# Row pads that shift the start bytes of operand tiles in a hybrid decoder trunk

## The chip, the cores and the metric

The kernel runs on one core of one Trainium2 chip, as one launch. The metric is the device time of that launch in microseconds, the median over repeated executions.

## The reference

Two layers (DEPTH 2) over 512 positions of width 1024, float32. Each layer computes an RMSNorm, one combined input projection, three groups of heads side by side (6 heads of differential attention, 4 groups of a short gated convolution, 6 heads of RWKV-7 time mixing), one output projection added to x, then a second RMSNorm and a squared-ReLU MLP of width 4096, added to x. A final RMSNorm follows.

```python
for l in range(DEPTH):
    h = rms_norm(x, norm_mix_g[l])
    proj = h @ w_in[l]
    p_att, p_conv, p_rwkv = jnp.split(proj, [3 * ATT_W, 3 * ATT_W + 3 * CONV_W], axis=-1)
    ...
    mixed = jnp.concatenate([o_att, o_conv, o_rwkv], axis=-1)
    x = x + mixed @ w_out[l]
    h = rms_norm(x, norm_mlp_g[l])
    x = x + jnp.square(jax.nn.relu(h @ w_mlp_up[l])) @ w_mlp_down[l]
return rms_norm(x, final_norm_g)
```

## The kernel before

x is held transposed, as 8 tiles `x[j]` of 128 partitions (features) by 512 positions. Every large product is taken at float32 precision in three matmuls: the weight block and the activation are each split into a rounded part (`hi`, type float32r) and a remainder (`lo`), and the product is whi x ahi + whi x alo + wlo x ahi (the function `mm3_steps`, and `passes` in the mixer). The activation is the moving operand of the matmul, 512 wide; the weight block of 128 x 128 is the stationary one. The split costs a copy on ACT and a subtraction on DVE or POOL for each weight half group (256 KB, loaded by SP's queue into `raw`) and each activation tile.

Stages of one layer, with the names that the profile uses:

- **Mixer.** `entry` (layer 1: also `scaled`, lines 401 to 407) writes the scaled input tiles `ahim`/`alom`. `products` runs the 26 groups of the input projection into `pj`. Attention (`sc`, `ptt`), RWKV (`pw`, `pa<-za`, `pg`, `pzw`, `pap` and others) and convolution are generators; a written-out list (ORDER) says which generator takes its next step, and this is the order on every engine. Matmuls of `pj` are put between the small matmuls of attention and RWKV. The decay products `pw` take the tiles `tw`, `to` as moving operands and `lkt`, `lvt` as weights. Results go to the mixed tiles `mhi`/`mlo` 0 to 7 (`mix_out`, line 846). The output projection `po` takes them in the order `K_ORD = (0, 5, 3, 1, 6, 4, 2, 7)` in two cuts of four: for each of the 8 output tiles first the tiles 0, 5, 3, 1, amid attention and RWKV work, and later, for each output tile, 6, 4, 2, 7, as one long stream.
- **Start of the MLP.** `inputs` writes `ahif`/`alof`, and the up projection `up` starts: 3 blocks within the mixer's list, then blocks up to 8.
- **MLP.** Of the 32 up blocks, 8 are plain (`up`) and 24 are taken as 12 pairs by the function `two`, which uses a 2 x 2 block scheme with 7 products instead of 8 (each 256 wide, 4 blocks deep, 12 matmuls): three of the products have as moving operand parts of the normed input (`bhi`/`blo`), four have combinations of them, the block tiles `thi`/`tlo`. The squared-ReLU results are the middle tiles `mh`/`ml`, in rings of 10, which the down projection `dn` (and `dnF` in the last group of layer 1) takes as moving operands. The order in this stage is the scheduler's, from the order in which the program is written.

All SBUF tiles come from pools that lay one tag behind the other, padded to 32 bytes per partition; tiles of one tag share a slot of the largest size. The map of the built program before the change (bytes within a partition):

| tiles | first start | step | start modulo 512 |
|---|---|---|---|
| `x0` to `x7` | 1,600 | 2,048 | 64 |
| tags `ahi0`, `alo0`, `ahi1`, ... `alo7`: `ahim`/`alom`, `mhi`/`mlo` of tiles 1, 2, 3, 4, 6, 7, `ahif`/`alof`, `bhi`/`blo` | 23,424 | 2,048 | 384 |
| `raw`, `whi`, `wlo` | 61,312 | 2,048 | 384 |
| `mh` ring, then `ml` ring | 98,176 | 2,048 | 384 |
| `thi0` to `tlo3`, with other tiles between | 163,712 | 4,096 and more | 384 |
| `tw`, `to`, `lkt`, `lvt` of layer 0 | 129,952 | 2,048 | 416 |
| mixed tiles 0 and 5 of layer 0 ("own" home, in the mixer's pool) | 210,336 and 216,480 | - | 416 |
| mixed tiles 0 and 5 of layer 1 | 218,528 and 212,320 | - | 416 and 352 |

The mixer's pool (`mp`) and the MLP's pool (`fp`) take turns in the same memory from 83,840 on; the mixer's ends at 228,800 before the change.

Of the kernel before, what the change touches and what calls it, by code (L numbers as in the profile page):

```python
# [11 lines left out]
F32R = mybir.dt.float32r  # L12
# [10 lines left out]
S = 512  # L23
P = 128
# [255 lines left out]
def tile_trunk(ctx: ExitStack, tc: tile.TileContext, xT, wts, prm_d, cst_d, lora_d, gup_d, lam_d, fin_d, out):  # L280
# [20 lines left out]
    cp = Pool(ctx.enter_context(tc.tile_pool(name="cp", bufs=1)), "cp")  # L301
# [119 lines left out]
    def got(d, k):  # L421

        while k not in d:
            yield
        return d[k]
# [4 lines left out]
    def entry(ready, l):  # L430

        for j in range(NK - LATE if l else 0, NK):
            yield from got(ready, ("x", j))
            gcol = prm[l][:, C_GMIX + j:C_GMIX + j + 1]
            hi = cp.tile([P, S], F32R, tag=f"ahi{j}", name=f"ahim{l}_{j}")
            lo = cp.tile([P, S], F32R, tag=f"alo{j}", name=f"alom{l}_{j}")
            acts[j] = (hi, lo)
            yield act.activation(hi, x[j], AF.Identity, scale=gcol)
            yield dve.scalar_tensor_tensor(lo, x[j], gcol, hi.bitcast(F32), ALU.mult, ALU.subtract)
# [132 lines left out]
    for l in range(L):  # L572
# [5 lines left out]
        with ExitStack() as mx:  # L578
# [652 lines left out]
            def att_pair(t):  # L1231
# [106 lines left out]
                for b in range(NB):  # L1338
# [6 lines left out]
            work = {"d": loads(), "w": casts(), "x": rests(dve), "y": rests(pool), "m": products(), "o": outputs(),  # L1345
                    "n": norm(), "g": rates(), "h": gate(), "i": inputs(), "p": squares(), "N": inner_norm()}
            work |= {"e": entry(ready, l), "q": entry_norm(ready, l)}
            if l == 0:
                work["k"] = constants(ready)
# [13 lines left out]
        with ExitStack() as mx:  # L1363
            fp = mx.enter_context(tc.tile_pool(name=f"fp{l}", bufs=1))
            RING = 10
            H = S // 2
# [4 lines left out]
            def kept(m):  # L1371

                i = len(mids)
                hi = fp.tile([P, S], F32R, tag="mh", bufs=RING, name=f"mh{l}_{i}")
                lo = fp.tile([P, S], F32R, tag="ml", bufs=RING, name=f"ml{l}_{i}")
                act.copy(hi, m)  # L1376
                pool.tensor_tensor(lo, m, hi.bitcast(F32), ALU.subtract)  # L1377
                mids.append((hi, lo))

            def square(cs, name):  # L1380

                r = fp.tile([P, S], F32, tag="r", bufs=2, name=f"r{name}")
                for i, c in enumerate(cs):
                    act.activation(r[:, i * H:i * H + c.shape[1]], c, AF.Relu)
                m = fp.tile([P, S], F32, tag="m", bufs=3, name=f"m{name}")
                act.activation(m, r, AF.Square)
                kept(m)
# [14 lines left out]
            bn, th = {}, {}  # L1402
# [6 lines left out]
            def blocks(k):  # L1409
                b1, b2 = bn[k], bn[k + 4]  # L1410
                t = [fp.tile([P, 2, H], F32, tag=f"s{2 * (k % 2) + i + 1}", name=f"t{l}_{k}_{i}") for i in range(2)]
                dve.tensor_tensor(t[0][:, 0], b1[:, 1], b1[:, 0], ALU.subtract)
                dve.tensor_tensor(t[0][:, 1], b2[:, 1], t[0][:, 0], ALU.subtract)
                dve.tensor_tensor(t[1][:, 0], b2[:, 1], b1[:, 1], ALU.subtract)
                dve.tensor_tensor(t[1][:, 1], b2[:, 0], t[0][:, 1], ALU.subtract)
                hi, lo = th[k] = [fp.tile([P, 4, H], F32R, tag=f"t{p}{k}", name=f"t{p}{l}_{k}") for p in ("hi", "lo")]
                for i in range(2):
                    u = slice(2 * i, 2 * i + 2)
                    act.copy(hi[:, u], t[i])
                    dve.tensor_tensor(lo[:, u], t[i], hi[:, u].bitcast(F32), ALU.subtract)  # L1420
# [89 lines left out]
            for i in range(N_ONE):  # L1510
                up(i)
                for j in range(2 * max(i - 2, 0), min(2 * max(i - 1, 0), NK)):
                    scaled_by_norm(j)
                if i >= N_ONE - 4:
                    blocks(i - N_ONE + 4)
# [79 lines left out]
```

## Time and profile before

| | |
|---|---|
| median of 3 runs | 1267.0 us (1266.56 to 1267.16) |
| profiled execution, its own time | 1266.47 us |
| its span, first to last instruction | 1264.7 us |
| mean granted clock of TensorE | 0.998 |
| PE busy | 1242.8 us, 9493 matmuls |
| DVE busy | 913.5 us |
| ACT busy | 696.9 us |
| POOL busy | 335.3 us |

The page lists instruction groups by line, engine, operation and tiles; all matmuls have the line of one helper (L289), so that they are told apart by their tiles (`dn<-ml,whi`: output, moving operand, weights). Matmuls overlap in the pipe: the duration of one is longer than the distance from its start to the next start, and it is the latter that adds up.

### The profile page before, as it was taken

How to read it: one execution, taken by the hardware profiler on the slowest of the kernel's cores; microseconds unless marked ns; L12 is line 12 of the kernel's file. 1: busy time of each engine (PE TensorE's matmuls, PEld its weight loads, DVE VectorE, ACT ScalarE, POOL GpSimd, SP SyncE). 2: the span in 40 equal slices, each digit the busy share in tenths (PEclk: the TensorE clock that was granted, in tenths of full speed). 3: DMA queues.
4: the chain of work that ended last, by engine and by line, in shares of the span. 5: the costliest groups of instructions: out<-in, count | busy, mean ns of one | idle time of the engine just before them, and what ended most of it. 6: DMA issues, size and time to landing. Idle time of an engine off the chain costs nothing.

```text
span 1264.7 us, 25145 instructions
## 1 busy us (share of the span) xinstructions
PE 1242.8 (98%) x9493; PEld 1051.4 (83%) x9493; DVE 913.5 (72%) x1889; ACT 696.9 (55%) x1474; POOL 335.3 (27%) x433
## 2 busy tenths in 40 slices
PE   9999999999999999999999999999999999999997
PEld 6777777787789898989878787787787989898987
DVE  6788888867966666765667787879598666666654
ACT  7675655646744544544575656564575545454553
POOL 1353626133300101010224335352431010111110
PEclk9999999999999999999999999999999999999999
DMA  6522333142333333321235333332424233333122
GB/s 212 159 84 94 109 94 101 52 134 83 103 122 101 101 101 100 101 84 51 75 103 146 98 102 110 98 97 60 134 92 133 93 107 96 106 98 103 59 74 77
DMA packets 84410, 127.93 MB, mean 101 GB/s; under 512 B 21440, under 2 KB 25024, under 8 KB 84288
## 3 DMA queue, kind: packets, MB, share of 16 engines
q1 hardware_dynamic: 83568, 125.77, 32.6%
q8 instruction: 75, 1.23, 0.4%
q10 hardware_dynamic: 720, 0.55, 0.1%
q14 instruction: 47, 0.39, 0.1%
HBM read 117.11 MB, written 9.18 MB: 100 GB/s over the span
## 4 chain that ended last, share of the span: by engine, by line
PE 70%; DVE 4%; issue 1%; ACT 1%; DMA 0%; POOL 0%; DVEq 0%; ACTq 0%; POOLq 0%
PE dn L289 22%; PE pj L289 11%; PE pa L289 11%; PE up L289 6%; PE pb L289 5%; PE po L289 4%; PE dnF L289 3%; PE pc L289 3%; PE sc L289 1%; PE ptt L294 1%; PE pg L289 1%; DVE wlo L343 0%; DVE blo L1429 0%; DVE x L1505 0%; PE pyy L289 0%
## 5 line engine op out<-in xcount | busy, mean ns | idle before, releaser
L1377 POOL TENSOR_TENSOR ml<-m,mh 128x512 fp32r<-128x512 f32 x64 | 95.2, 1489 | 510.8 <-ACT mh L1376 510.6
L342 ACT CAST whi<-raw 128x512 fp32r<-128x512 f32 x142 | 88.1, 621 | 174.1 <-PE dn L289 158.5
L289 PE MATMUL dn<-mh,whi 128*128 128x512 f32 x448 | 175.3, 391 | 1.9 <-DVE x L1505 1.9
L289 PE MATMUL dn<-ml,whi 128*128 128x512 f32 x448 | 174.6, 390 | 0.0
L289 PE MATMUL dn<-mh,wlo 128*128 128x512 f32 x448 | 174.4, 389 | 0.0
L289 PE MATMUL pj<-ahim,whi 128*128 128x512 f32 x392 | 157.7, 402 | 4.4 <-DVE vf L1266 1.7
L289 PE MATMUL pj<-ahim,wlo 128*128 128x512 f32 x392 | 158.3, 404 | 0.0
L289 PE MATMUL pj<-alom,whi 128*128 128x512 f32 x392 | 158.2, 404 | 0.0
L662 ACT CAST whi<-raw 128x512 fp32r<-128x512 f32 x142 | 87.7, 619 | 93.6 <-PE pj L289 40.4
L671 POOL TENSOR_TENSOR wlo<-raw,whi 128x512 fp32r<-128x512 f32 x62 | 81.7, 1317 | 214.5 <-ACT whi L662 198.3
L1505 DVE TENSOR_TENSOR x<-dn,x 128x512 f32<-128x512 f32 x112 | 76.8, 686 | 76.8 <-PE dn L289 76.8
L343 DVE TENSOR_TENSOR wlo<-raw,whi 128x512 fp32r<-128x512 f32 x142 | 115.2, 812 | 11.4 <-ACT whi L342 10.7
L1444 DVE TENSOR_TENSOR slo_p<-s,shi_p 128x512 fp32r<-128x512 f32 x96 | 70.9, 740 | 63.6 <-ACT shi_p L1443 58.9
L289 PEld LDWEIGHTS dn<-mh,whi 128*128 128x128 f32 x448 | 84.2, 188 | 21.3 <-ACT whi L342 2.4
L289 PEld LDWEIGHTS dn<-mh,wlo 128*128 128x128 f32 x448 | 84.1, 188 | 17.8
L289 PEld LDWEIGHTS dn<-ml,whi 128*128 128x128 f32 x448 | 84.2, 188 | 16.5
L289 PEld LDWEIGHTS pj<-ahim,whi 128*128 128x128 f32 x392 | 73.9, 188 | 19.8 <-issue 1.7
L1443 ACT CAST shi_p<-s 128x512 fp32r<-128x512 f32 x96 | 59.2, 618 | 51.2 <-PE pa L289 39.1
L289 PEld LDWEIGHTS pj<-ahim,wlo 128*128 128x128 f32 x392 | 73.8, 188 | 14.3 <-issue 0.9
L289 PEld LDWEIGHTS pj<-alom,whi 128*128 128x128 f32 x392 | 73.8, 188 | 14.1 <-issue 0.5
L289 PE MATMUL pa<-thi,shi_p 128*128 128x256 f32 x288 | 81.6, 283 | 0.2 <-DVE c L1489 0.2
L289 PE MATMUL pa<-thi,slo_p 128*128 128x256 f32 x288 | 81.5, 283 | 0.0
(409 smaller groups left out, 3264.5 us busy)
## 6 DMA issues: line engine op xcount, KB each, us to landing
raw<-wts SPq DMA_DIRECT2D x391, 256.0 KB, 2.7
qs<-dqhi SPq DMA_DIRECT2D x24, 128.0 KB, 3.3
ks<-dkhi SPq DMA_DIRECT2D x24, 128.0 KB, 3.8
x<-xT SPq DMA_DIRECT2D x8, 256.0 KB, 5.0
dqhi<-qhi SPq DMA_DIRECT2D x6, 256.0 KB, 3.3
dqlo<-qlo SPq DMA_DIRECT2D x6, 256.0 KB, 2.8
dkhi<-khi SPq DMA_DIRECT2D x6, 256.0 KB, 2.6
dklo<-klo SPq DMA_DIRECT2D x6, 256.0 KB, 2.9
```

The lines of the kernel that those rows point to most:

```text
L289: ins = nc.tensor.matmul(*a, **k)
L294: ins = nc.tensor.transpose(*a, **k)
L342: act.copy(hi[:, :n], raw[:, :n])
L343: (pool if a and lean[0] else dve).tensor_tensor(lo[:, :n], raw[:, :n], hi[:, :n].bitcast(F32), ALU.subtract)
L662: yield act.copy(hi[:, k0:k1], raw[:, k0:k1])
L671: yield eng.tensor_tensor(lo[:, :n], raw[:, :n], hi[:, :n].bitcast(F32), ALU.subtract)
L1377: pool.tensor_tensor(lo, m, hi.bitcast(F32), ALU.subtract)
L1443: act.copy(hi, src)
L1444: dve.tensor_tensor(lo, src, hi.bitcast(F32), ALU.subtract)
L1505: dve.tensor_tensor(x[j], pt, x[j], ALU.add)
```

## The change

Three kinds of tiles get a pad at the end of each row, and a view without the pad is used in their place. Shapes, values, instructions and their order as written stay.

- The input tiles `ahim`/`alom` written by `entry` have 520 elements, 2,080 bytes (were 512 and 2,048). Their tags `ahi0` to `alo7` are shared by all tiles of the second row of the table above, and a slot has the size of its largest tile.
- The middle tiles `mh`/`ml` have 528 elements, 2,112 bytes.
- The block tiles `thi`/`tlo` have 1,040 elements, 4,160 bytes (were 1,024 and 4,096).

```diff
@@ entry
-            hi = cp.tile([P, S], F32R, tag=f"ahi{j}", name=f"ahim{l}_{j}")
-            lo = cp.tile([P, S], F32R, tag=f"alo{j}", name=f"alom{l}_{j}")
+            hi = cp.tile([P, S + 8], F32R, tag=f"ahi{j}", name=f"ahim{l}_{j}")[:, :S]
+            lo = cp.tile([P, S + 8], F32R, tag=f"alo{j}", name=f"alom{l}_{j}")[:, :S]
@@ kept
-                hi = fp.tile([P, S], F32R, tag="mh", bufs=RING, name=f"mh{l}_{i}")
-                lo = fp.tile([P, S], F32R, tag="ml", bufs=RING, name=f"ml{l}_{i}")
+                hi = fp.tile([P, S + 16], F32R, tag="mh", bufs=RING, name=f"mh{l}_{i}")[:, :S]
+                lo = fp.tile([P, S + 16], F32R, tag="ml", bufs=RING, name=f"ml{l}_{i}")[:, :S]
@@ blocks
-                hi, lo = th[k] = [fp.tile([P, 4, H], F32R, tag=f"t{p}{k}", name=f"t{p}{l}_{k}") for p in ("hi", "lo")]
+                hi, lo = th[k] = [fp.tile([P, 4 * H + 16], F32R, tag=f"t{p}{k}", name=f"t{p}{l}_{k}")[:, :4 * H].rearrange("p (i s) -> p i s", s=H)
+                                  for p in ("hi", "lo")]
```

## The prediction

> **What bounds the kernel now.** I read the page first, then the groups with shapes kept apart, the waits of PE, the chain, and the timeline of PE alone around the second layer's output projection.
>
> ```profile
> span 1264.7 us, 25145 instructions
> PE 1242.8 (98%) x9493; PEld 1051.4 (83%) x9493; DVE 913.5 (72%) x1889; ACT 696.9 (55%) x1474; POOL 335.3 (27%) x433
> PEclk9999999999999999999999999999999999999999
> 369.47 10.91 PE dn L289 x48
> ...
> PE ptt L294 <- DVE pp L1311: 2.7, 4, 0.9
> ...
> 335.00:632.00 297.00, 295.78 (x1774) 1.00 0.30 94
> 632.00:908.00 276.00, 272.99 (x2712) 1.00 0.36 106
> 908.00:954.00 46.00, 45.85 (x209) 1.00 0.29 92
> ...
> L289 PE MATMUL dn<-mh,whi 128*128 128x512 f32 x448 | 175.3, 391 | 1.9 <-DVE x L1505 1.9
> L289 PE MATMUL dn<-ml,whi 128*128 128x512 f32 x448 | 174.6, 390 | 0.0
> L289 PE MATMUL dn<-mh,wlo 128*128 128x512 f32 x448 | 174.4, 389 | 0.0
> ```
>
> PE is busy 98% of the span, at full granted clock. The chain's piece of 48 down matmuls takes 10.91 us, 227 ns from start to start, with nothing between them; the stretches (layer 0's MLP, layer 1's mixer, layer 1's first up projections) have 295.78 of 297 us, 272.99 of 276 and 45.85 of 46 covered. PE's longest group of waits for another engine sums to 2.7 us. So the end is set by what one matmul costs PE; a change of addresses counts if it alters that, and otherwise hardly at all. Busy durations overlap (389 to 391 ns of one `dn` matmul at a pitch of 227), so I go by start times.
>
> **Does the start byte of a moving operand alter it?** The trace has no addresses, but the old map has a natural experiment. Nearly every operand of the long streams starts at 384 modulo 512, a multiple of 64. The exceptions include the mixed tiles 0 and 5 of layer 1 (own home: 416 and 352) and the decay inputs `tw`, `to` with their weights (416): 32 past a multiple of 64. In `po` the order of tiles is 0, 5, 3, 1, three matmuls each. Here is PE's timeline (start us, duration us):
>
> ```profile
> 876.32 0.39 PE L289 MATMUL po<-mhi,whi 128*128 128x512 f32 x1
> ...
> 877.71 0.40 PE L289 MATMUL po<-mhi,whi 128*128 128x512 f32 x1
> ...
> 879.10 0.40 PE L289 MATMUL po<-mhi,whi 128*128 128x512 f32 x1
> 879.34 0.39 PE L289 MATMUL po<-mlo,whi 128*128 128x512 f32 x1
> ...
> 880.47 0.40 PE L289 MATMUL po<-mhi,whi 128*128 128x512 f32 x1
> ...
> 881.64 0.40 PE L289 MATMUL po<-mhi,wlo 128*128 128x512 f32 x1
> ```
> ```profile
> 35.87 0.39 PE L289 MATMUL pj<-ahim,whi 128*128 128x512 f32 x1
> 36.10 0.40 PE L289 MATMUL pj<-alom,whi 128*128 128x512 f32 x1
> 36.33 0.39 PE L289 MATMUL pw<-tw,lkt 128*128 128x512 f32 x1
> 36.56 0.39 PE L289 MATMUL pw<-to,lvt 128*128 128x512 f32 x1
> 36.79 0.39 PE L289 MATMUL pj<-ahim,wlo 128*128 128x512 f32 x1
> ...
> 37.48 0.39 PE L289 MATMUL pj<-ahim,wlo 128*128 128x512 f32 x1
> 37.71 0.39 PE L289 MATMUL pj<-ahim,whi 128*128 128x512 f32 x1
> ```
>
> Three matmuls go to each tile; those at 876.32 and 879.10 begin with tile 3, those at 877.71 and 880.47 with tile 0. From 879.34 the stream is in step: five starts to 880.47 in 1.13 us, 226 ns each. Then tiles 0 and 5 come, and five starts to 881.64 take 1.17 us, 234 each: 35 ns over 5 x 227, **7 ns each**. The six from 877.71 to 879.10 take 1.39 us, 232 each, which by itself proves little, since the six aligned ones before them, from 876.32 just behind an attention batch, took 1.39 too: a stream that was interrupted runs out of step for a while wherever its operands lie. In the second fence two such operands stand in an undisturbed stream: 36.10 to 37.71 is seven starts in 1.61 us, 21 ns over 1.589: **10 ns each**, of which part falls on the aligned ones behind, as if the stream needed several matmuls to find its step again. (Their weights are 32 off too, so 10 is on the high side for the moving operand.) Starts are rounded to 10 ns.
>
> [...]
>
> **The change part by part.** *Where things land.* Old map: `ahi0` at 23,424, then `alo0`, `ahi1` and so on, all multiples of 64. With slots of 2,080 bytes `ahi_j` moves by 4,160 j, still a multiple of 64; every `alo_j` is now 32 past one. The slots go by tag, so all tenants move: `alom` (layer 1's tiles from `scaled` too), `mlo` of the six mixed tiles in this pool, `alof`, and `blo` in the block products. All 16 pads add 512 bytes, so what lies behind keeps its byte of 512; the attention's pool then ends at 229,312. The middle tiles step by 64 and the block tiles by 64: multiples of 64 stay so, half of them now 64 past a multiple of 128. *What is added:* no instruction, no DMA, no wait; the pads are never written.
>
> How many matmuls read a tile moved to 32 past 64:
>
> ```profile
> L289 PE MATMUL pj<-alom,whi 128*128 128x512 f32 x392 | 158.2, 404 | 0.0
> L289 PE MATMUL pj<-alom,whi_s 128*128 128x512 f32 x24 | 9.6, 400 | 0.3 <-DVE alom L439 0.3
> L289 PE MATMUL up<-alof,whi 128*128 128x512 f32 x128 | 50.6, 395 | 0.0
> L289 PE MATMUL po<-mlo,whi 128*128 128x512 f32 x128 | 50.8, 397 | 0.0
> L289 PE MATMUL pa<-blo,shi_p 128*128 128x256 f32 x96 | 27.2, 283 | 0.0
> L289 PE MATMUL pb<-blo,shi_p 128*128 128x256 f32 x96 | 27.2, 283 | 0.0
> L289 PE MATMUL pc<-blo,shi_p 128*128 128x256 f32 x96 | 27.2, 283 | 0.0
> ```
>
> Each stands alone between two aligned ones (hi, lo, hi). A lone one is in no row. Bounds: 7 ns at the low end, if only the operand itself costs; at the high end its own 7 plus the loss of step. Of the pair's 21 ns, 14 is two operands and 7 the loss of step, so 14 for a lone one; with 10 ns of rounding in the row, up to 20. The pattern returns every third matmul, before the stream is back in step, so I take **13 ns per triple** in undisturbed streams.
>
> - `pj`: 392 + 24 = 416. These run between attention and RWKV matmuls: 404 ns of one against 390 for `dn` shows a stream that is mostly out of step already, where the second cost is paid anyway. Half: 6.5 x 416 = 2.7 us.
> - `up`: 128 x 13 = 1.7 us.
> - `po`: six of eight tiles, 96 of 128. 64 in the quiet second half at 13, 32 in the broken first half at 6.5: 1.0 us.
> - `blo`: 96 + 96 + 96 = 288 at 13 = 3.7 us. No row shows a 256-wide one; I take the 512-wide price, as an extra that hangs on the start does not scale with length. From below, 0 for `pa`, `pb`, `pc` if a shorter stream hides it.
> - `ahi`, middle and block tiles: 0, as they stay multiples of 64. Nothing hides a cost here (the stretches are covered by PE); if 64 past 128 counts, see the second rival.
> - Writers: ACT's copies, DVE's and POOL's subtractions land on shifted slots. The low mixed tiles lie at both kinds of start before the change, and DVE writes them alike:
>
> ```profile
> L852 DVE TENSOR_TENSOR mlo<-om,mhi x6: 671/693/694, 130.3 to 886.6; 128x512 fp32r<-128x512 f32 x6
> L1377 POOL TENSOR_TENSOR ml<-m,mh 128x512 fp32r<-128x512 f32 x64 | 95.2, 1489 | 510.8 <-ACT mh L1376 510.6
> ```
>
>   671 to 694 ns for minimum and maximum over both kinds; POOL's group sits idle 510.8 us before its 64 pieces, which would cover a slower write. 0.
> - Reuse of memory between the mixer's pool and the MLP's: the overlaps move by 0.5 to 2.3 KB, so a first write may wait for another old tile. The tiles concerned are mostly dead; PE's row of waits (2.7 us in its largest group) bounds it, from -2.7 to +2.7 us; I take 0, as the streams before and after the seams are nearly covered.
>
> Sum: 2.7 + 1.7 + 1.0 + 3.7 = 9.1 us. The profiled execution took 1266.47 us (span 1264.7 and 1.8 around it), 0.5 below the median of 1267.0; 1266.5 + 9.1 = 1275.6, on the median's footing 1276.1. **Forecast 1276.0 us**, slower by 0.7%. Its own range: low, 7 ns for the 512-wide ones of `up` and `po` alone, 224 x 7 = 1.6 us: 1268.6. High, 20 ns for all 928: 18.6 us, 1285.6. A gain from the starts themselves is excluded where the stream is in step already, as `dn` is; what remains of a gain is the third rival.
>
> **Rivals.** *Nothing happens (not slower).* The slow stretches are only tails of interruptions, and start bytes are free. For: 876.32 to 877.71, aligned and as slow. Against: 880.47 to 881.64 follows five matmuls at 226, and the pair at 36.33 stands in a quiet stream. Then 1267.0, within 2.5 us. [...] Chance 0.13.
>
> *64 past 128 counts as well.* The block products read `tlo` in
>
> ```profile
> L289 PE MATMUL pa<-tlo,shi_p 128*128 128x256 f32 x288 | 81.5, 283 | 0.0
> L289 PE MATMUL pb<-tlo,shi_p 128*128 128x256 f32 x96 | 27.2, 283 | 0.0
> ```
>
>   384 matmuls, and `tlo` is the half of the block tiles that comes to lie at 64 past 128; of the three kinds of `dn` with 448 each, half are 672. At 7 to 13 ns these 1,056 add 7 to 14 us: 1283 to 1290, central 1287. For: the old streams lie on multiples of 128 alike, so the trace cannot exclude it. Against: no tile at 64 past 128 runs in a long stream; the few short ones look like their neighbours. Chance 0.15.
>
> *The spread relieves a conflict (faster).* DVE's subtraction of weights takes longer in the MLP than in the mixer:
>
> ```profile
> L343 DVE TENSOR_TENSOR wlo<-raw,whi 128x512 fp32r<-128x512 f32 x142 | 115.2, 812 | 11.4 <-ACT whi L342 10.7 <-PE up L289 0.6
> L671 DVE TENSOR_TENSOR wlo<-raw,whi 128x512 fp32r<-128x512 f32 x80 | 56.3, 705 | 5.9 <-ACT whi L662 5.3 <-PE pb L294 0.2
> ```
>
>   812 against 705 ns, 15 us over 142. If equal bytes of 512 were the reason and the change cured it, PE would gain only what it waits for: at most the 2.7 us of its largest group. 1264.3. Against: weights and raw tiles keep equal bytes of 512, and PE's pitch in `dn` is already constant. Chance 0.04, decided where PE waits for DVE.
>
> **How the numbers follow.** The forecast has 0.68, the second rival 0.15. Both are slower by over 0.2% (2.5 us, about what a measurement of this kernel can tell from no change), but for 0.02 at the forecast's low end: 0.81. Within: 0.13 + 0.02 = 0.15. Faster: 0.04. The range leaves out at most 2 in 10: from 1267.0, which keeps half of "nothing happens" (0.07) and nearly all of the forecast's case (0.67), to 1288, which keeps half of the second rival (0.07): 0.81.
>
> **What would show it.** Right: start-to-start in the `up` stretch of layer 1 rises from 227 to about 231 ns, in `pa<-bhi`/`blo` products by 4 to 5 ns a matmul, the mean duration of `up<-alof` from 395 to 398 or more, and `dn` stays at 227 with 48 in 10.91 us. `dn` above that means the second rival. All pitches as before means the first. Wrong also, if DVE or POOL durations of `alof`, `ml` or `tlo` move by more than 5% and PE begins to wait for them. An idle PE at the starts of the MLP pools would be the reuse of memory that I put at 0.

## The result, and the profile after

| | before | after |
|---|---|---|
| median | 1267.0 us (5 runs beside it, 1266.56 to 1267.55) | 1272.8 us (5 runs, 1271.97 to 1272.92) |
| span of the profiled execution | 1264.7 us | 1270.5 us |
| ratio to before | 1 | 1.0044, 95% interval 1.0029 to 1.0059 |

The change makes the kernel 5.8 us slower. The order of the matmuls is the same in both programs, so every row below compares like with like. First, of the changed kernel, the head of the page, PE's largest group of waits, two stretches (length, time covered by PE, matmuls), and groups of instructions (busy us, mean ns of one, idle before).

```profile
span 1270.5 us, 25145 instructions
PE 1249.9 (98%) x9493; PEld 1048.1 (82%) x9493; DVE 915.2 (72%) x1889; ACT 696.8 (55%) x1474; POOL 334.4 (26%) x433
...
PE ptt L294 <- DVE pp L1311: 2.6, 4, 0.8
...
335.00:632.00 297.00, 296.62 (x1771) 1.00 0.30 94
632.00:908.00 276.00, 273.02 (x2705) 1.00 0.36 106
...
L289 PE MATMUL dn<-mh,whi 128*128 128x512 f32 x448 | 177.3, 396 | 0.4 <-DVE x L1506 0.3
L289 PE MATMUL dn<-ml,whi 128*128 128x512 f32 x448 | 176.3, 394 | 0.0
L289 PE MATMUL pj<-alom,whi 128*128 128x512 f32 x392 | 159.0, 406 | 0.0
L289 PE MATMUL pa<-tlo,shi_p 128*128 128x256 f32 x288 | 80.5, 280 | 0.0
L289 PE MATMUL up<-alof,whi 128*128 128x512 f32 x128 | 51.2, 400 | 0.0
L343 DVE TENSOR_TENSOR wlo<-raw,whi 128x512 fp32r<-128x512 f32 x142 | 115.4, 813 | 11.5 <-ACT whi L342 10.9 <-PE up L289 0.6
L1377 POOL TENSOR_TENSOR ml<-m,mh 128x512 fp32r<-128x512 f32 x64 | 95.7, 1498 | 512.7 <-ACT mh L1376 494.3 <-PE pa L289 18.1 <-POOL ml L1377 0.3
```

PE's busy time grew by 7.1 us, its largest group of waits did not (2.6 us, was 2.7), and the writers nearly kept their durations (813 ns, was 812; 1498, was 1489). The same stretch holds fewer matmuls (1771, were 1774). The `dn` rows rose from 389 to 391 ns to 394 to 396, the 256-wide `pa<-tlo` row fell from 283 to 280.

The MLP repeats a cycle of 48 down matmuls (512 wide) and seven block products (84 matmuls, 256 wide). The chain of waits shows each batch (start us, length us); first the kernel before, then the changed one:

```profile
390.95 10.91 PE dn L289 x48
...
411.93 10.91 PE dn L289 x48
```
```profile
392.81 11.13 PE dn L289 x48
...
413.88 11.17 PE dn L289 x48
```

A cycle took 20.98 us and takes 21.07. The `dn` part went from 10.91 to 11.13; what is left, the block products, went from 10.07 to 9.94. **The two kinds moved in opposite directions.**

Taken from start to start over all matmuls of the trace (us of the whole kernel, after less before; each matmul has the time up to the next start): `dn` +4.5, `pj` +2.4, `up` +1.2, `po` +0.9, the 512-wide part of `dnF` +0.6; products of `bhi`/`blo` -1.7, of `thi`/`tlo` -1.4, the 256-wide part of `dnF` -0.3; the rest -0.2. Sum +6.0, against 5.8 by the spans.

In quiet streams (eight matmuls of the same width ahead) the kernel before has a pitch, the time from start to start, of 226.7 ns at 512 wide and 120.0 at 256, nearly constant. The changed one scatters around 232.0 (`dn`) and 118.4.

### The profile page after: what moved, and what is told of

It is laid out like the page before. It is cut to its first block, busy times and chain, and to the rows that moved or that the text cites. A ratio compares the mean times of both kernels' runs of the same rounds, so it can differ in the third digit from the quotient of the medians.

```text
span 1270.5 us, 25145 instructions
## 1 busy us (share of the span) xinstructions
PE 1249.9 (98%) x9493; PEld 1048.1 (82%) x9493; DVE 915.2 (72%) x1889; ACT 696.8 (55%) x1474; POOL 334.4 (26%) x433
## 4 chain that ended last, share of the span: by engine, by line
PE 72%; DVE 3%; issue 1%; ACT 1%; DMA 0%; POOL 0%; DVEq 0%; ACTq 0%; POOLq 0%
PE dn L289 23%; PE pj L289 11%; PE pa L289 11%; PE up L289 6%; PE pb L289 5%; PE po L289 4%; PE dnF L289 3%; PE pc L289 3%; PE sc L289 1%; PE ptt L294 1%; PE pg L289 1%; PE pyy L289 0%; DVE x L1506 0%; DVE o L533 0%; PE pst L289 0%
## 5 line engine op out<-in xcount | busy, mean ns | idle before, releaser
L1377 POOL TENSOR_TENSOR ml<-m,mh 128x512 fp32r<-128x512 f32 x64 | 95.7, 1498 | 512.7 <-ACT mh L1376 494.3
```

## The experiments

All numbers called start to start come from the trace of the run; start bytes come from the map of the built program. The first four kernels do one part of the change each, or move everything alike.

### One part alone, and everything by 32 bytes

```diff
# x1_input: the two lines of entry only        [P, S + 8]
# x2_middle: the two lines of kept only        [P, S + 16]
# x3_block: the line of blocks only            [P, 4 * H + 16]
# x4_shift32: none of them, but the last tile ahead of ahi0 is 32 bytes longer
-nlam = cp.tile([P, L], F32, tag="nlam", name="nlam")
+nlam = cp.tile([P, 16], F32, tag="nlam", name="nlam")[:, :L]
```

> The input pads alone (slots of 2,080 bytes); middle and block tiles as before. A (the prediction's): an operand that starts 32 bytes past a multiple of 64 costs by itself, so this alone brings the whole predicted 9 us: 1276, with up and the blo products slower. B (a change of the start byte from one moving operand to the next is what costs): the change's own trace has pj 2.4 + up 1.2 + po 0.9 us more and the products on bhi/blo 1.6 us less: 1270. C (the distance between the start of the moving operand and that of the weights): as B here, 1270.

> The middle pads alone (slots of 2,112 bytes, all multiples of 64). A: no operand comes to lie 32 past 64, so 1267.0 and dn at 227 ns. B: dn 4.4 us and dnF 0.6 us more, as in the change: 1272, and the 256-wide products stay at 120 ns although they have all moved by 256 bytes of 512 together, but for the input blocks, which keep their place. C: dn as in B, and the products on bhi/blo, whose weights now start 256 bytes away from them, leave 120 ns.

> The block pads alone (slots of 4,160 bytes; thi and tlo 64 bytes apart modulo 512). A: 1267.0. B and C: the products on thi/tlo go from 120 to about 118.6 ns, as in the change, 1152 of them: 1.5 us less, 1265.5.

> No pad, but a small tile ahead of the input tiles is 32 bytes larger, so that all input, weight, middle and block tiles start at 416 modulo 512 in place of 384: all alike, and all 32 past a multiple of 64. A: 7 ns for each of some 3,500 512-wide and 2,100 256-wide matmuls, about 40 us: 1307. B and C: nothing changes between neighbours, nor between moving operand and weights: 1267.0, pitch 227 and 120 ns.

Measured beside 1267.06 us of before (`b`: products on `bhi`/`blo`; `th`: on `thi`/`tlo`):

| run | us | ratio, 95% interval | what moved, start to start (us) |
|---|---|---|---|
| x1_input | 1267.17 | 0.9998, 0.9989 to 1.0006 | `pj` +2.3, `up` +1.2, `po` +0.9; `b` products -1.9, `th` products -0.4, `dn` -1.1 |
| x2_middle | 1273.24 | 1.0047, 1.0033 to 1.0061 | `dn` +5.5, `dnF` +0.6 (512 wide) and -0.3 (256 wide), `pj` +1.0; block products 0 |
| x3_block | 1264.17 | 0.9978, 0.9968 to 0.9988 | `th` -1.9, `b` -0.7, `dnF` -0.4 (256 wide; its weights lie in the slots of the block tiles); `pj` +1.2 |
| x4_shift32 | 1267.14 | 1.0001, 0.9992 to 1.0010 | `pj` +1.3, the small matmuls +1.1; `dn`, `up`, `po`, block products 0 |

Two batches of `dn` in the chain of x4_shift32, in which every operand of `dn`, `up`, `pj` and the block products starts 32 past a multiple of 64:

```profile
391.03 10.91 PE dn L289 x48
...
412.01 10.91 PE dn L289 x48
```

10.91 us and a cycle of 20.98, as before the change. **Theory A, the prediction's, falls**: a start 32 past a multiple of 64 has no price by itself here (1267.14 us beside 1267.06). The loss sits in the middle tiles, which the prediction put at 0; the input tiles' +4.4 us (1270 was expected by the other theories) are paid back by 2.3 in the block products and by 1.1 in `dn`, which I can't name a reason for; the block tiles alone make the kernel faster. The parts add to +3.4 us (+0.1, +6.2, -2.9), the whole is +5.8. Most of the difference of 2.4 is that the gains at 256 wide overlap: input and block tiles alone bring -1.9 - 0.4 - 1.9 - 0.7 - 0.4 = -5.3 us there, in the whole they are -3.4.

What was left was some relation between starts. I held theory B (a change of start from one moving operand to the next), because x2_middle left the block products with moving operands at 384 and weights at 128 of 512 at 120.0 ns, which spoke against theory C (the distance between moving operand and weights).

### Which relation: period, weights, size of the step

```diff
# x5_mid256: middle tiles 2,304 bytes apart    [P, S + 64]
# x6_weights: whi and wlo 2,112 bytes apart; the tile acc ahead of them is 128 bytes
# longer, so that what lies behind keeps its byte of 512
-[wp.tile([P, 4, P], F32R, tag="w" + p, bufs=WB, ...) for p in ("hi", "lo")]
+[wp.tile([P, 4 * P + 16], F32R, tag="w" + p, bufs=WB, ...)[:, :4 * P].rearrange("p (k c) -> p k c", c=P) for p in ("hi", "lo")]
# x7_block32: block tiles 4,128 bytes apart    [P, 4 * H + 8]
# x8_blo: x7_block32, and the low parts blo begin at other bytes than bhi
+if j < 4:
+    lo = cp.tile([P, 2 * H], F32R, tag=f"alo{j}", ...)[:, 16:16 + H]...
+elif j == 7:
+    lo = cp.tile([P, 2 * H + 128], F32R, tag=f"alo{j}", ...)[:, 16:16 + 2 * H]...
+else:
+    lo = fp.tile([P, 2 * H + 8], F32R, tag=f"blo{j}", ...)[:, 8:]...
```

> Middle tiles alone, 2,304 bytes apart: consecutive ones begin at 384 and 128 modulo 512, alternately (a change of 256). B (a change of start from one moving operand to the next breaks the locked pitch) in its form with period 512: dn as with 64-byte steps, 230.3 -> about 234 ns mean, +4 to +6 us, 1272. B with period 256: nothing changes, dn at 230.3, 1267.1 within 1.5. What speaks for 256 so far: in the kernel with padded middle tiles a block product between operands at 384 and 128 stayed at 120.0 ns. The prediction's theory (a price on the start itself) would also give 1267, but it has fallen with the common shift.

> Stationary tiles whi and wlo alone, 2,112 bytes apart (0, 64, 128, 192, 256, 320 modulo 512, one another per tile); all moving operands where they were before. B (moving operands alone count): pitches unchanged, dn 230.3, up 238.0, pj 250.4, time 1267.1 within 1.5. Rival D (the weight load's start counts in the same way, hi after hi after lo): dn +3 to +5 ns, up and po +3, pj +2: +5 to +8 us, 1272 to 1275. Rival C (distance between the moving start and the weights' start): as D, but also a change where only that distance differs: every dn, up, po and pj matmul with it, 1272 or more. The weights of the 256-wide products are other tiles and stay: th and b at 120.1 in each theory.

> Block tiles alone, 4,128 bytes apart (steps of 32, were 64 in the run of block tiles alone, 1264.2). B: any change of start sets the 256-wide stream free; within a triple (hi, lo, hi) the change is +32, -32, then +32 or +64. In the run of input tiles alone the products with changes of -32 and +64 had 115 to 118 ns. So th 120.1 -> 117.3 (1152 x 2.8 = 3.2 us) and b -0.7 us: 1263.2. If the size of the step does not matter: th 118.4 as with 64, 1264.2. If a change of 32 is too small to count (a period or grain of 64): th 120.1, 1267.1. dn, pj, up, po unchanged in each.

> Block tiles 4,128 bytes apart as in the run beside it, and the low parts blo moved as well, without moving any 512-wide operand: blo 0 to 3 and 7 by a view that begins 64 bytes further in their old slots (448 modulo 512), blo 4 to 6 in tiles of their own (160, 192, 224); bhi stays at 384. B: b 120.3 -> about 118 (864 x 2.3 = 2.0 us) beside th at 117.3 to 118.4: 1261 to 1262. If b cannot be set free beside hi tiles at one byte: no gain over the run beside it, 1263 to 1264. The prediction's theory would make it slower than 1267.

Measured beside 1266.85 us of before: x5_mid256 1266.95 (ratio 1.0000, 0.9991 to 1.0009); x6_weights 1276.74 (1.0077, 1.0064 to 1.0089); x7_block32 1263.54 (0.9974, 0.9963 to 0.9984); x8_blo 1263.55 (0.9973, 0.9963 to 0.9983). The chain of x5_mid256, and that of x6_weights:

```profile
391.17 10.91 PE dn L289 x48
...
412.15 10.91 PE dn L289 x48
```
```profile
392.98 11.13 PE dn L289 x48
...
414.18 11.11 PE dn L289 x48
```

Steps of 256 bytes cost `dn` nothing: 10.91 and 20.98 again, so the period there is 256 and not 512. That also takes away the evidence against C: 384 and 128 lie 256 apart. And **the weights count**: with no moving operand touched, `dn` rose by 4.6 us, `pj` by 2.9, `up` by 1.4, `po` by 1.2, and the block products, whose weights are other tiles, stayed at 120.0 in quiet streams. B, which knows moving operands only, is not enough.

x7_block32 brought `th` from 120.1 to 117.6 ns (-2.9 us), about as expected; its `b` products, expected 0.7 us lower, did not move. x8_blo gained nothing over it: its `b` products fell by 0.7 us in the trace instead of the expected 2.0, while `pj`, which it doesn't touch, shows +1.6. What one trace shows of `pj`, from -0.3 to +1.8 us over kernels that leave its tiles in place, is no effect of theirs that I could name; the sums of `pj` given here are uncertain by as much.

### A constant distance

Now nothing changes within a stream; only the distance between moving operands and weights is other than 0.

```diff
# x9_dist64: D = 64; x10_dist128: D = 128; x11_dist192: D = 448
-c = fp.tile([P, S], F32, tag="c0", bufs=2, name=f"c{l}_{i}")
+c = fp.tile([P, S + D // 8], F32, tag="c0", bufs=2, name=f"c{l}_{i}")[:, :S]
# two slots of D/2 more ahead of the middle tiles and of shi/slo;
# a scratch tile behind them (t, k even, i = 1) 512 - D longer, so that thi/tlo stay
```

> All middle tiles begin at 448 modulo 512 (were 384), all weights of the 256-wide products too; everything else, the weights of dn and the moving operands of the 256-wide products among it, stays at 384. So the distance from a moving operand to its weights is 64 everywhere in dn and in the block products, and nothing changes from one matmul to the next. Theory B+D (changes of start in either stream break the locked pitch; distance is free): dn 230.3, th and b 120.1, 1267.1 within 1.5. Rival C (the distance modulo 256 between moving start and weights' start decides; the padded kernels were slow because their distances differ): dn and the 256-wide products get another pitch. By the padded middle tiles' rows at distance 64 (230.8 against 226.7 in long streams) dn +4 ns or +5 us; by the padded block tiles' rows at 64 (119.0) the 256-wide ones -1 to -2 ns or -2 to -4 us: 1268 to 1270 by C, with up, po and pj unchanged in both.

> As the run beside it with 128 in place of 64: middle tiles and the weights of the 256-wide products begin at 0 modulo 512, the others at 384. B+D: 1267.1 within 1.5, no pitch moves. C: dn by the rows at distance 128 (231.3) +4.6 ns or +6 us, the 256-wide ones by theirs (117.9, and 115.2 with steps of 32) -2 to -5 ns or -4 to -10 us: 1263 to 1269, with dn and th visibly off 230.3 and 120.1. up, po and pj unchanged in both.

> The mirror of the run at 64: middle tiles and the weights of the 256-wide products begin at 320 modulo 512, 64 bytes ahead of the others at 384. Distance from moving operand to weights (moving start less weights' start, modulo 256): 192 in dn (was 64 there), 64 in the block products th and b (was 192 there). Theory C (this distance, constant, sets the pitch), if only its size counts: dn 232.5 as at 64, th and b 116 to 117.5, 1263. C with a sign that counts: dn and the 256-wide pitches change places in their order: a value of their own, 512-wide anywhere from 225 to 236 ns and 256-wide from 114 to 120 in quiet streams, 1258 to 1272. If instead the shift of the MLP's pool as a whole, or its other tiles, made the difference at 64: no reason for either value, and th and b back at 120.1. up, po, pj unchanged.

x9_dist64 took 1262.94 us (ratio 0.9965, 0.9954 to 0.9975), x10_dist128 1273.30 (1.0054, 1.0042 to 1.0067), x11_dist192 1270.60 (1.0027, 1.0016 to 1.0039), before 1266.9 to 1267.0. In this order, two batches of each chain:

```profile
411.81 10.98 PE dn L289 x48
...
432.51 10.98 PE dn L289 x48
```
```profile
412.66 11.20 PE dn L289 x48
...
433.94 11.15 PE dn L289 x48
```
```profile
392.05 11.20 PE dn L289 x48
...
413.15 11.20 PE dn L289 x48
```

Cycles of 20.70, 21.28 and 21.10 us (20.98 before). Less the `dn` part that leaves 9.72, 10.08 and 9.90 for the block products. With all starts constant along each stream, the pitch of `dn` moved in all three, and that of the block products in x9_dist64 and x11_dist192 (10.07 us before; x10_dist128 leaves it nearly as it was). **For constant streams theory C holds, modulo 256, and B falls as the whole cause.** B, also with a price on changes of the weights' start (D of the expectations), gave 1267.1 us here. `up` and `po`, in which no distance changed, kept 238.0 to 238.1 and 241.4 to 241.5 ns in all three. Start to start in quiet streams, means in ns, from the five kernels with constant distance:

| moving start less weights' start, modulo 256 | 512 wide (`dn`) | 256 wide (block products) |
|---|---|---|
| 0 | 226.7 (before, x12) | 120.0 (before) |
| 64 | 229.5 (x9: batches at 228.9, some at 233.3) | 117.8 (x11) |
| 128 | 232.7 (x10) | 119.5 (x10) |
| 192 | 233.4 (x11) | 114.2 (x9: most products at 113.3, some at 117.8), 117.8 (x12, the last run below) |

My sizes missed for x9 (1268 to 1270 expected: I took them from scattered streams) and x10 (1263 to 1269).

In x9_dist64 one product stands out. Six of the seven block products of this cycle take 1.36 to 1.39 us (1.36 is 113.3 ns a matmul), and the last takes longer. The end of a cycle in the chain, and the timeline around the start of its last product:

```profile
429.63 1.36 PE pb L289 x12
430.99 1.53 PE pa L289 x12
```
```profile
429.35 0.28 PE L289 MATMUL pa<-thi,slo_p 128*128 128x256 f32 x1
429.35 0.19 PEld L289 LDWEIGHTS pb<-bhi,shi_p 128*128 128x128 f32 x1
...
430.39 0.42 DVE L1490 TENSOR_TENSOR c<-pa,p 128x256 f32<-128x256 f32 x1
...
430.71 0.28 PE L289 MATMUL pb<-bhi,slo_p 128*128 128x256 f32 x1
...
430.87 0.19 PEld L289 LDWEIGHTS pa<-thi,shi_p 128*128 128x128 f32 x1
430.87 0.38 PE L289 MATMUL pa<-thi,shi_p 128*128 128x256 f32 x1
...
431.09 0.29 PE L289 MATMUL pa<-tlo,shi_p 128*128 128x256 f32 x1
```

The last product's first matmul comes 0.16 us behind its predecessor instead of 0.11, just after DVE's `c` ended at 430.81, and the next one another 0.22 later: it looks as if PE had become fast enough to wait for DVE there, which no run tested. When the weights of a matmul are loaded also shows: the load starts with the matmul ahead (both at 429.35, and in `dn` of the kernel before both at 372.05). So a load could disturb the moving operand of the matmul ahead, which is a guess from these times. Where all weights of a stream start at one byte modulo 256, this can't be told from the distance to a matmul's own weights. In x6_weights they differ: there the `dn` matmuls of quiet streams take 229.3, 232.1, 232.8 and 233.7 ns at distances 0, 64, 128 and 192 from their own weights, in the order of the table, but 230.9, 231.3, 233.6 and 229.5 by the distance from the weights that are loaded beside them. That the distance counts is shown, why it does is not.

### The kernel that the table points to

```diff
# x12_weights256: shi and slo begin 64 bytes further, nothing else
-[fp.tile([P, 4, P], F32R, tag=f"s{p}", bufs=5, ...) for p in ("hi", "lo")]
+[fp.tile([P, 4 * P + 128], F32R, tag=f"s{p}", bufs=5, ...)[:, 16:16 + 4 * P].rearrange("p (k c) -> p k c", c=P) for p in ("hi", "lo")]
```

> Only the weights of the 256-wide products (shi and slo) move: each begins 64 bytes further in its slot, at 448 modulo 512; all moving operands and the weights of dn, up, pj and po stay at 384. Distance 192 in the block products, 0 in every 512-wide stream. Theory C: th 120.1 -> 116.1 and b 120.3 -> 117.5 as in the run with middle tiles at 64 (quiet streams 114.2), -4.6 and -2.4 us, dn back at 230.3: 1260 within 1.5, the fastest of all. If the gain there needed the middle tiles' shift too, or if a 512-wide stream loses its pitch for some matmuls behind a faster 256-wide one: dn up to 232.5 (+2.9 us), 1263. If distance is not the cause: 1267.

Two batches of `dn` in its chain, and the two products behind the second:

```profile
391.24 10.90 PE dn L289 x48
...
412.04 10.90 PE dn L289 x48
422.94 1.42 PE pa L289 x12
424.36 1.41 PE pb L289 x12
```

1263.10 us (ratio 0.9968, 0.9955 to 0.9980), faster than both kernels, but not the 1260 expected. `dn` is back at 10.90, as C says; the products take 1.41 us, 117.8 ns a matmul (-2.5 and -1.3 us), not the 1.36 of x9_dist64 at the same distance of 192. So **the distance alone does not fix the 256-wide pitch**: in x9 the `dn` batches between the products ran at distance 64, here at 0. That alone does not decide it, as the chain of x9_dist64 shows:

```profile
360.78 1.41 PE pb L289 x12
...
369.26 11.01 PE dn L289 x48
...
424.19 1.36 PE pb L289 x12
...
473.87 11.20 PE dn L289 x48
```

The first two groups of seven products, and the last two of layer 0, run at 117.8 ns behind `dn` batches at 64, the others mostly at 113.3; `dn` itself has batches of 10.98 and of 11.20 us there. The page of x9_dist64 has the granted clock at 9, its highest digit, in every slice up to 1230 us, which holds all of these stretches. The 256-wide part of `dnF` likewise has stretches near 113 and near 118 ns at distance 64 (x9) and at 192 (x11). So a stream at one constant distance can settle at more than one pitch, and what picks it stays open. That streams act on each other would fit two more sums: in x3_block the products on `bhi`/`blo` kept their distance of 0 and yet fell from 120.3 to 119.4 ns, and in x1_input `dn` fell by 1.1 us.

Four kernels end within 1262.9 to 1263.6 us (x7, x8, x9, x12); these runs give no order among them.

## Why the prediction was right or wrong

The direction came out, and the time lay within the range (1276.0 forecast, 1272.8 measured; 9.1 us more forecast, 5.8 measured), but for a reason that was wrong. Of the prediction's own signs two came: `up` of layer 1 at 231.4 ns in quiet streams, and `up<-alof` at 400 ns. Two did not: `dn` went from 10.91 to 11.13 us, and the products on `bhi`/`blo` got 1.9 ns faster, not 4 to 5 slower.

- **What bounds the kernel**: right. PE's pitch sets the time (PE is busy 98% of the span in both), PE's waits stayed (2.6 us in the largest group, was 2.7), and a change of addresses counted through that pitch.
- **The natural experiment**: seen rightly, read wrongly. Tiles 0 and 5 at 416 and 352 lay 32 bytes from their weights at 384 modulo 256; I called the 7 ns a price of the start byte, although the weights' start stood in the same map. x4_shift32 gives that price as 0. The pair `tw`, `to`, whose own weights were 32 off too, does not fit its own distance of 0; the weights loaded beside it lie at 384, which would fit if these counted, but x6_weights speaks against that, and no run tried the pair.
- **`pj`, `up`, `po`** (2.7, 1.7, 1.0 us): measured 2.4, 1.2 and 0.9 in the changed kernel, 2.3, 1.2 and 0.9 with the input tiles alone. The sums came near (that of `pj` is hardly clear of its scatter of up to 1.8), but the step to them failed: it charged the low parts alone, 32 past a multiple of 64. By the map `ahi` moved to 0, 64, 128 and 192 from its weights and `alo` to 32, 96, 160 and 224, and all three matmuls of a triple paid: in `up` 2.8, 4.8 and 2.1 ns, in `po` 2.0, 2.6 and 2.4. That 13 ns on one of three came near these sums is luck.
- **`blo`** (3.7 us): the step "an extra that hangs on the start does not scale with length" failed, and the sign with it. The 256-wide products got 1.7 us faster; the lower bound of 0 excluded that for a reason that holds for a stream at its minimum. 120.0 was not one: x9_dist64 has 113.3. It is also this pitch (`th` at 117.6 ns in x7_block32, was 120.1) that made x3_block and x7_block32 faster, not the shorter wait for DVE of the third rival.
- **Middle and block tiles** (0): `dn` +4.5 and `dnF` +0.6 us, `th` -1.4 us. The second rival, 64 past 128, had the place for `dn` and about the size per matmul (5 ns in quiet streams), but the wrong sign for `tlo`, and x6_weights and x10_dist128 show that it is no rule of its own: in both no moving operand of `dn` starts 64 past a multiple of 128, and `dn` is slower all the same. It is the distance to the weights that became 64, 128 or 192.
- **Writers and reuse** (0): right, by the rows of `wlo` (813 ns, was 812) and `ml` (1498, was 1489) and PE's waits.

So the sum of 9.1 came within some 3 us of the measured 5.8 by luck: the 512-wide terms of `pj`, `up` and `po` (5.4 forecast, 4.5 measured) came near by a wrong step, and +3.7 for `blo` stood where +5.1 (`dn`, `dnF`) and -3.4 (all 256-wide) belonged.

**Open**: `dn` with mixed distances was slower than the table makes it. The four distances of `dn` in the changed kernel, weighted by their counts (313, 328, 262, 282) with the table's values, give 230.4 ns; measured are 232.0. Sorted by its own distance, a `dn` matmul there takes 232.8 ns at 0, 230.7 at 64, 231.5 at 128 and 233.1 at 192: at 0, 6 ns more than in a constant stream. So the table holds for constant streams, and the loss of the changed kernel can't be added up from it; a price on the change from one matmul to the next, theory B's, may come on top.

## What to carry to other kernels

Where PE is bound by back-to-back matmuls with a fresh weight load each, as here, first try moving operands and weights whose starts agree modulo 256 all along the 512-wide streams: `dn` took 226.7 ns so, and 229.5, 232.7 and 233.4 at distances of 64, 128 and 192. The 256-wide streams here were faster at other distances, constant (117.8 ns in x12_weights256, 120.0 before) or mixed (117.6 in x7_block32, 120.1 before), so measure them by moving the weights alone. Before pricing a start byte, ask what it is relative to: a kernel in which all operands move alike separates an absolute price from a distance in one run (x4_shift32: 10.91 us a batch of `dn`, as before). And when a term of the sum is set to 0 or bounded below by 0, check that the stream is at its minimum already.

## What the runs showed of the hardware

- The distance between the starts of the moving operand and of the weights, modulo 256 bytes, moved the mean pitch of 128x128 float32r matmuls in quiet streams: 226.7 to 233.4 ns at 512 wide, 114.2 to 120.0 at 256 wide (before, x9_dist64 to x12_weights256). A common shift of 32 bytes and steps of 256 bytes left the pitch of `dn` and the block products as it was (x4_shift32 and x5_mid256: 10.91 us a batch of `dn` and a cycle of 20.98 in both; 1267.14 and 1266.95 us).
- Of the constant distances tried (0, 64, 128, 192), 0 is the best at 512 wide (226.7 ns) and the worst at 256 wide (120.0).
- At one constant distance a stream can settle at more than one pitch: in x9_dist64 at 113.3 and 117.8 ns at 256 wide, at 228.9 and 233.3 at 512 wide.
